# The opening of a decoder-block kernel, rebuilt: column sums by matmul, two tiles loaded in pieces, 13 short constant products

## The chip, the core and the metric

One core of a Trainium2 chip runs one program. Its engines work at the same time and wait for one another by semaphores: PE (TensorE, matmuls; PEld is its weight load), DVE (VectorE), ACT (ScalarE), POOL (GpSimd) and SP (SyncE, which here only issues DMAs). The metric is the device time of one execution in microseconds (us), as the median of several runs. Lower is better.

## The reference, cut to what matters

One decoder block on 256 tokens of width 2048, all in float32:

```python
mod = silu(c) @ w_ada + b_ada                 # (1, 6 * 2048)
sh1, sc1, g1, sh2, sc2, g2 = split(mod, 6)
h = rms_norm(x, norm1_g) * (1 + sc1) + sh1    # (256, 2048)
proj = h @ w_in                               # (256, 6144): q, k, v, gb, gc, xt
...                                           # attention, short convolution, w_out,
...                                           # then a gated ConvFFN with w_ffn_up, w_ffn_down
```

The change touches only the way to the first product of `h @ w_in`: the first 256 columns of `sc1` and `sh1`, the transposed normed x, and the first weight tile.

## The kernel before

Weights come from HBM in tiles of 1 MB ("raw", 128 rows x 2048 floats). All of them are issued by SP in one fixed order into a ring of buffers, so they land in that order: x (two tiles), four tiles of `w_ada` for the opening (the scale's columns 0 to 255 in two tiles of 8 row blocks, then the shift's), then the first weight tile of `w_in` in two halves, and from there `w_in` tiles with `w_ada` tiles between them. The `w_ada` tiles of the opening go through PE (L396, `ada<-raw,crep`), later ones through PE or through DVE (L387 and L389).

A product that is nearly exact in float32 is made of three fast ones: each weight tile is split into a rounded part `hi` (ACT, L329) and a rest `lo` (DVE, `lo<-raw,hi`), each h chunk into `h` and its rest, and PE computes hi·h, hi·(rest of h) and lo·h. The work is cut into slots, one weight tile each; slot 0 is `mc`, slot 1 `mv`, slot 2 `mg`, slot 3 `mx`, slots 4 and 5 `mq`. Within a slot hi comes first. Slots 0 to 4 multiply the first two h chunks (columns 0 to 255 of x), slot 5 is the first that needs chunks 2 and 3, whose parts are named `h` and `hl`. Each engine carries out its instructions in program order. The trace shows two passes (x16) for eight float32 products through `ada`, which the order of the instructions shows as x8. The splits of a slot stand two slots ahead of it.

The opening (L1470 to L1560): PE transposes x (`xn<-ident,xr`). DVE multiplies each transposed pair by the inverse norm (`xn_norm`, `xnT<-xn,n1rT`, eight of them). PE sums silu(c) times the scale's tiles into four groups of 32 rows (`Ada.consume`); ACT copies the sums out (`adae`, `Ada.evac`), PE transposes the copy and DVE adds the four groups up (`adac`, `adaz`, `Ada.cols`). The shift takes the same way after it. Then `hf` (DVE) is the normed x scaled, and `h` (ACT) is `hf` plus the shift column `z`, rounded. The first product `mc` needs `h` and the first piece of `hi`. In the program text `hf` stands behind all eight `xn_norm`.

Of the kernel before, what the change touches and what calls it, by code (L numbers as in the profile page):

```python
# [28 lines left out]
SH1, SC1, G1, SH2, SC2, G2 = range(6)  # L29
# [118 lines left out]
def tile_block(  # L148
# [22 lines left out]
    V, W = Vector(), nc.vector  # L171
# [5 lines left out]
    const = ctx.enter_context(tc.tile_pool(name="const", bufs=1))  # L177
# [4 lines left out]
    def bank(name):  # L182
        return ps.tile([P, 512], F32, tag="b", bufs=8, name=name)
# [30 lines left out]
    ident = const.tile([P, P], F32, name="ident")  # L214
# [3 lines left out]
    onesr = const.tile([P, P], F32R, name="onesr")  # L218
# [121 lines left out]
    crep = const.tile([P, NK, 32], F32, name="crep")  # L340
    A1 = const.tile([P, NK], F32, name="A1")
# [4 lines left out]
    class Ada:  # L346


        def __init__(self, part, c0, n, pe):
            self.part, self.c0, self.n, self.pe = part, c0, n, pe  # L350
            self.rows = 2048 // n
            self.tiles = NK // self.rows
            self.nch = n // P
            self.acc = None
            self.two = []
            self.used = 0

        def want(self, r):
            a = self.part * D + self.c0 * P
            k0 = r * self.rows  # L360

            def issue(t):
                nc.sync.dma_start(self.view(t), w_ada[0, k0 * P:(k0 + self.rows) * P, a:a + self.n]
                                  .rearrange("(k p) f -> p k f", p=P))
            return issue

        def home(self):
            what = f"ada{self.part}_{self.c0}"
            self.acc = sb.tile([P, 4, 512], F32, tag="raw", bufs=N_RAW, name=what).rearrange("p a b -> p (a b)")

            nc.gpsimd.memset(self.acc, 0.0)
            a = self.part * D + self.c0 * P
            nc.gpsimd.dma_start(self.acc[0:1, :], b_ada[0:1, a:a + self.n])
# [114 lines left out]
    hT = {}  # L488
# [31 lines left out]
    for w in CFG["parked"]:  # L520
        q = sb.tile([P, 4, 512], F32, tag="raw", bufs=N_RAW, name="pa_" + w)
# [15 lines left out]
    slots_begun = []  # L537

    def pair_load(k, f):
        def issue(t):  # L540

            n = 1 if not slots_begun else 2
            slots_begun.append(f)
            for j in range(0, 2, n):
                nc.sync.dma_start(t.rearrange("p (k h) f -> p k (h f)", k=2)[:, j:j + n],
                                  w_in[0, (k + j) * P:(k + j + n) * P, COL[f] * 512:COL[f] * 512 + 1024]
                                  .rearrange("(k p) f -> p k f", p=P))
        return issue


# [125 lines left out]
    for n, (f, part, k) in enumerate(seq):  # L676
# [6 lines left out]
        i = len(slots)  # L683
# [411 lines left out]
    for n, (what, *a) in enumerate(CFG["plan"]):  # L1095
        if what == "x":
# [10 lines left out]
            rest = todo  # L1107
# [12 lines left out]
    parts = []  # L1120
    for fs in CFG["down_turns"]:
        k = ka
# [46 lines left out]
        ready_at.update({(g.part, g.c0 + k): s + 2 for k in range(g.nch)})  # L1169

    ada_init = [Ada(SC1, 0, 256, True), Ada(SH1, 0, 256, True)]

    def h_chunks(ks):
        assert all((part, k) in done for k in ks for part in (SC1, SH1))

        for k in ks[::2]:
            t, hi, lo = t2k("hf"), t2k(f"h{k}", F32R), t2k(f"hl{k}", F32R)
            for j in range(2):
                s = slice(j * 256, (j + 1) * 256)
                act(t[:, s], xnT[k // 2][:, s], AF.Identity, scale=A1[:, k + j:k + j + 1], bias=B1[:, k + j:k + j + 1])  # L1180
                hT[k + j] = hi[:, s], lo[:, s]
            act(hi, t, AF.Copy)
            V.tensor_tensor(out=lo, in0=t, in1=hi.bitcast(F32), op=ALU.subtract)
# [268 lines left out]
    for i in range(len(slots)):  # L1452
# [3 lines left out]
        w = [("w", n) for n in ahead(i)]  # L1456
# [11 lines left out]
    for t in range(2):  # L1468
        r = sb.tile([P, 4, 512], F32, tag="hi", bufs=N_HL, name="xr").rearrange("p a b -> p (a b)")
# [16 lines left out]
    xnT, xnP = {}, {}  # L1486
# [26 lines left out]
    def xn_norm(*js):  # L1513
        for j in js:
            xnT[j] = t2k(f"xnT{j}")
            V.tensor_tensor(out=xnT[j].rearrange("p (k t) -> p k t", k=2), in0=xnP.pop(j).rearrange("p (k t) -> p k t", k=2),
                            in1=rT.unsqueeze(1).to_broadcast([P, 2, 256]), op=ALU.mult)

    xn_norm(0, 1, 2, 3)
    ada_init[0].consume(1)  # L1520
    ada_init[0].evac()
    ada_init[0].cols()
    xn_norm(4)
    xn_tr(5)
    ada_init[1].consume(0)
    xn_tr(6, 7)
    xn_norm(5, 6, 7)
    ada_init[1].consume(1)
    ada_init[1].evac()

    w = take(("w", 0))
    hi, lo = (sb.tile([P, 4, 512], F32R, tag=g, bufs=N_HL, name=g) for g in ("hi", "lo"))
    parts = [(slice(2 * k, 2 * k + 2), t1k("hf"), t2k(f"h{k}", F32R)) for k in range(2)]
    b1 = SH1 * NK
    for k, (s, h, hk) in enumerate(parts):
        hT[k] = halves(hk)
        V.tensor_scalar(h, xnT[0][:, k * 256:(k + 1) * 256], A1[:, k:k + 1], bcol[:, b1 + k:b1 + k + 1],
                        op0=ALU.mult, op1=ALU.add)  # L1540
    s = parts[0][0]
    if CFG["first_hi"]:
        V.tensor_copy(hi[:, s], w[:, s])
    else:
        act(hi[:, s], w[:, s], AF.Copy)
    z, _ = ada_init[1].cols(True)
    for k, (s, h, hk) in enumerate(parts):
        act(hT[k][0], h, AF.Identity, bias=z[:, k:k + 1])
# [38 lines left out]
    for i in range(len(slots)):  # L1587
# [28 lines left out]
        hi, lo = splits.pop(0)  # L1616
# [42 lines left out]
```

## Time and profile before

| | |
|---|---|
| median of three runs (lowest to highest) | 1145.96 us (1145.74 to 1147.56) |
| the profiled execution: its time, its span from first to last instruction | 1145.98 us, 1144.2 us |
| mean granted TensorE clock | 0.997 |
| bytes read from HBM, mean rate | 343.70 MB, 317 GB/s over the span |

Times in the trace count from the span's start; what lies around the span is 1145.98 − 1144.2 = 1.8 us. "PEclk" in a row is the share of the TensorE clock that was granted in that stretch. "DMA" is the mean busy share of the 16 DMA engines. A bracket behind a row gives the engine's idle time before it and what ended it. In the last column of a DMA row stands the time from the issue to the landing, in us.

### The profile page before, as it was taken

To read this page: it belongs to the slowest core of one execution; us is meant where nothing else is said; L and a number is where in the kernel's file an instruction comes from. 1 tells how busy PE (TensorE), PEld (TensorE's weight loads), DVE (VectorE), ACT (ScalarE), POOL (GpSimd) and SP (SyncE) were. 2 spreads that over 40 slices of the span, in tenths; PEclk is the share of its full clock that TensorE was granted. 3 is DMA by queue.
4 is the path that set the end of the run, shared out by engine and by line. 5 is a ranking of instruction groups with operands and counts; after the bars stand their busy time and mean duration, and the time that the engine had idled before them with its cause. 6 is when DMAs were issued, how large, how long until landed. Compare 5 with 4: busy or idle time off the path is not lost.

```text
span 1144.2 us, 16252 instructions
## 1 busy us (share of the span) xinstructions
PE 1129.7 (99%) x6035; PEld 954.1 (83%) x6035; DVE 1064.4 (93%) x1167; ACT 731.6 (64%) x1091; POOL 61.5 (5%) x90
## 2 busy tenths in 40 slices
PE   6999999999999999999999999999999999999998
PEld 4777778888888879988888888888888888888887
DVE  4789989989999998889999999899999999999798
ACT  4644455576786555566687676776677768866731
POOL 1000000000000000000000000101011101111000
PEclk8999999999999999999999999999999999999999
DMA  9999998998998899987679887999899988999951
GB/s 361 407 412 397 412 371 302 408 382 308 331 397 314 290 317 359 325 278 245 213 246 369 305 293 248 310 360 299 313 272 340 317 317 265 351 313 303 367 222 74
DMA packets 198687, 363.66 MB, mean 318 GB/s; under 512 B 9408, under 2 KB 108180, under 8 KB 194000
## 3 DMA queue, kind: packets, MB, share of 16 engines
q1 hardware_dynamic: 189152, 343.44, 82.8%
q0 software_dynamic: 8160, 17.04, 6.9%
q10 hardware_dynamic: 1296, 2.16, 0.6%
q8 instruction: 47, 0.77, 0.2%
q14 instruction: 32, 0.26, 0.1%
HBM read 343.70 MB, written 18.89 MB: 317 GB/s over the span
## 4 chain that ended last, share of the span: by engine, by line
PE 94%; DVE 2%; DMA 2%; issue 1%; ACT 1%; SPq 0%; DVEq 0%; ACTq 0%
PE z L1063 24%; PE z L1066 13%; PE u L1002 4%; PE u L1004 4%; PE u L1000 4%; PE z L1048 4%; PE ada L396 1%; DVE lo L166 1%; PE mx L516 1%; PE mq L516 1%; PE mg L516 1%; PE mk L516 1%; PE mx L517 1%; PE mv L516 1%; PE mg L517 1%; PE mq L517 1%
## 5 line engine op out<-in xcount | busy, mean ns | idle before, releaser
L329 ACT ACTIVATE hi<-raw 128x2048 fp32r<-128x2048 f32 (+1 forms) x227 | 417.6, 1857 | 263.6 <-DMA raw<-in_w_in_dram 73.5
L166 DVE TENSOR_TENSOR lo<-raw,hi 128x2048 fp32r<-128x2048 f32 (+2 forms) x229 | 501.6, 2200 | 23.3 <-ACT hi L329 23.1
L1063 PE MATMUL z<-h,hi 128*128 128x512 f32 x1280 | 303.3, 390 | 0.3 <-DVE ub L166 0.3
L1063 PEld LDWEIGHTS z<-h,hi 128*128 128x128 f32 x1280 | 237.8, 188 | 49.5 <-ACT hi L329 0.8
L389 DVE SCALAR_TENSOR_TENSOR ada<-raw,csil,ada 128x512 f32<-128x512 f32 (+3 forms) x167 | 195.7, 1175 | 5.3 <-DMA raw<-in_w_ada_dram 1.8
L1066 PEld LDWEIGHTS z<-h,lo 128*128 128x128 f32 x1280 | 163.1, 191 | 5.6
L1066 PE MATMUL z<-h,lo 128*128 128x256 f32 x1280 | 165.0, 283 | 0.0
L1002 PE MATMUL u<-hi,gh 128*128 128x512 f32 x224 | 88.1, 394 | 0.1
L1004 PE MATMUL u<-hi,gl 128*128 128x512 f32 x224 | 87.7, 392 | 0.0
L1000 PE MATMUL u<-lo,gh 128*128 128x512 f32 x224 | 61.4, 390 | 0.0
L812 ACT ACTIVATE uy<-ub,fc,fc 128x256 f32<-128x256 f32 x88 | 47.6, 599 | 11.9 <-DVE ub L166 11.9
L944 POOL DMA_DIRECT2D down_sums<-pu x42 | 36.7, 1290 | 304.3 <-ACT pu L940 304.3
L1002 PEld LDWEIGHTS u<-hi,gh 128*128 128x128 f32 x224 | 42.2, 188 | 10.0 <-ACT pu L940 2.9
L1000 PEld LDWEIGHTS u<-lo,gh 128*128 128x128 f32 x224 | 41.9, 188 | 9.2 <-DVE lo L166 0.3
L1004 PEld LDWEIGHTS u<-hi,gl 128*128 128x128 f32 x224 | 42.2, 189 | 7.5
L1048 PE MATMUL z<-h,hi 128*128 128x256 f32 x256 | 46.6, 284 | 0.4 <-ACT h L771 0.2
L823 ACT ACTIVATE tap<-ub,fc 128x256 f32<-128x256 f32 x96 | 41.7, 504 | 0.0
L1048 PEld LDWEIGHTS z<-h,hi 128*128 128x128 f32 x256 | 40.0, 192 | 0.8 <-ACT h L771 0.5
L166 DVE TENSOR_TENSOR ub<-z,ub 128x256 f32<-128x256 f32 x96 | 33.8, 414 | 7.2 <-ACT ub L844 7.1
L301 DVE TENSOR_TENSOR raw<-raw 128x1024 f32<-128x1024 f32 x32 | 38.9, 1217 | 1.2 <-DMA raw<-in_w_ffn_down_dram 1.2
L844 ACT ACTIVATE ub<-z 128x256 f32<-128x256 f32 x96 | 28.6, 383 | 12.7 <-PE z L1063 12.7
L1048 PE MATMUL z<-h,lo 128*128 128x256 f32 x128 | 36.2, 283 | 0.0
(460 smaller groups left out, 1787.3 us busy)
## 6 DMA issues: line engine op xcount, KB each, us to landing
raw<-in_w_ada_dram SPq DMA_DIRECT2D x96, 1024.0 KB, 7.4
raw<-in_w_ffn_up_dram SPq DMA_DIRECT2D x176, 512.0 KB, 6.1
raw<-in_w_in_dram SPq DMA_DIRECT2D x47, 1024.0 KB, 8.1
raw<-in_w_ffn_down_dram SPq DMA_DIRECT2D x44, 1024.0 KB, 9.5
raw<-in_w_out_dram SPq DMA_DIRECT2D x16, 1024.0 KB, 5.9
raw<-in_w_ffn_down_dram SPq DMA_DIRECT2D x32, 512.0 KB, 4.9
down_sums<-pu POOLq DMA_DIRECT2D x56, 256.0 KB, 8.0
raw<-in_w_ffn_down_dram SPq DMA_DIRECT2D x32, 256.0 KB, 5.3
```

What stands on the lines that cost most here:

```text
L166: f(*a, **k)
L329: act(hi[:, :n], t[:, :n], AF.Copy)
L389: W.scalar_tensor_tensor(out=self.acc, in0=t[:, j, :], scalar=csil[:, i:i + 1], in1=self.acc, op0=ALU.mult, op1=ALU.add)
L516: mm(o, a, hi[:, k, s], start=(first and k == 0), stop=False)
L812: act(y[:, s], b[:, s], AF.Identity, bias=bias[:, i + j:i + j + 1], scale=w[2][:, i + j:i + j + 1])
L823: act(z[:, s], b[:, s], AF.Copy, scale=w[2 - d][:, i + j:i + j + 1])
L1000: mm(bank_of(key), a, lo[:, n], start=False, stop=j in ends)
L1002: mm(bank_of(key), a, hi[:, n], start=key not in begun, stop=False)
L1004: mm(bank_of(key), b, hi[:, n], start=False, stop=False)
L1048: mm(o, w[:, j, a], h2T[k + j][:, v * 256:v * 256 + 256], start=begins and j == 0 and w is hi and not v, stop=ends and j == 3 and w is lo)
L1063: mm(zp[grp][ft], hi[:, j, ft * P:(ft + 1) * P], h2T[k + j], start=begins and j == 0, stop=ends and j == 3 and not late)
L1066: mm(zp[grp][ft][:, :256], lo[:, j, ft * P:(ft + 1) * P], h2T[k + j][:, :256], start=False, stop=ends and j == 3 and late)
```

## The change

1. **Column sums of the shift.** Before: ACT copies the sums out, PE transposes two blocks of 128 x 128, DVE adds four columns of each, and ACT adds the result to `hf`. Now: ACT copies the sums out, PE multiplies the copy by a 0/1 column `sel` (two matmuls of one column each, into the bank `one`), DVE copies the two columns to `z`, and the first `h` is made by DVE, the second by ACT. `sel` is made at the start by one DVE reduction.
2. **Last shift tile in two DMAs** of four row blocks each, and its 8 products in two groups of four, each behind its own DMA.
3. **First weight tile in four DMAs** of 128 x 512 instead of two of 128 x 1024, and its `hi` in four casts by ACT, DVE, ACT, DVE instead of two.
4. **13 constant products** of 128 x 128 (`onesr` by itself, into an unused part of `one`): nine behind the first scale tile, four behind the second.
5. **DVE's order.** `hf` stands behind the second `xn_norm` instead of behind the eighth, and the eighth `xn_norm` stands behind the casts.

First place, PE from the first scale tile (`ada<-raw,crep`) to the scale's transposes (`adac`); `n1b` spreads the inverse norm over the partitions, `one<-onesr` are the constant products. Before:

```order
L396 MATMUL ada_0_165<-raw,crep 32x256 x8
L1509 MATMUL n1b<-n1d,ones 128x128 x2
L396 MATMUL ada_0_165<-raw,crep 32x256 x8
L453 MATMUL adac_0_206<-ident,adae_0_203 128x128 x2
L1495 MATMUL xn_214<-ident,xr 128x128 x4
```

The same stretch of PE now:

```order
L416 MATMUL ada_0_170<-raw,crep 32x256 x8
L1532 MATMUL one<-onesr 128x128 x9
L1541 MATMUL n1b<-n1d,ones 128x128 x2
L416 MATMUL ada_0_170<-raw,crep 32x256 x8
L1532 MATMUL one<-onesr 128x128 x4
L473 MATMUL adac_0_221<-ident,adae_0_218 128x128 x2
L1519 MATMUL xn_237<-ident,xr 128x128 x4
```

Nine constant products came in ahead of `n1b` and four ahead of `adac`; the rest stands as it stood.

Second place, PE from the last transposes of x to the first products of slot 0 (`mc`), before:

```order
L1495 MATMUL xn_233<-ident,xr 128x128 x2
L396 MATMUL ada_0_219<-raw,crep 32x256 x8
L453 MATMUL adac_0_268<-ident,adae_0_256 128x128 x2
L583 MATMUL mc_293<-hi,h_261 128x512
L583 MATMUL mc_294<-hi,h_261 128x512
```

The same stretch now (`one<-sel,adae` are the new column sums):

```order
L1519 MATMUL xn_256<-ident,xr 128x128 x2
L381 MATMUL ada_0_242<-raw,crep 32x256 x8
L1575 MATMUL one<-sel,adae 128x1 x2
L606 MATMUL mc_313<-hi,h_285 128x512
L606 MATMUL mc_314<-hi,h_285 128x512
```

The two transposes of 128 x 128 became two products of one column; PE's list is the same from `mc` on.

Third place, DVE from the scale's column sums (`adaz<-adac`) to the rests of the first two h chunks (the rows `h_261<-hf,adaz,h_261` and its like), before:

```order
L166 TENSOR_REDUCE adaz<-adac_0_206 128x2
L166 SCALAR_TENSOR_TENSOR adaz<-adaz,vbc 128x2
L166 TENSOR_TENSOR A_90<-adaz,vbc 128x2
L166 TENSOR_TENSOR xnT_212<-xn_139,n1rT 128x512
L166 TENSOR_TENSOR xnT_240<-xn_214,n1rT 128x512
L166 TENSOR_TENSOR xnT_242<-xn_230,n1rT 128x512
L166 TENSOR_TENSOR xnT_244<-xn_233,n1rT 128x512
L166 TENSOR_SCALAR hf<-xnT_185,A_90,vbc 128x256 x2
L166 CAST hi<-raw 128x1024
L166 TENSOR_REDUCE adaz<-adac_0_268 128x2
L166 SCALAR_TENSOR_TENSOR h_261<-hf,adaz,h_261 128x256
L166 SCALAR_TENSOR_TENSOR h_263<-hf,adaz,h_263 128x256
```

The same stretch now, up to the rest of the first chunk:

```order
L168 TENSOR_REDUCE adaz<-adac_0_221 128x2
L168 SCALAR_TENSOR_TENSOR adaz<-adaz,vbc 128x2
L168 TENSOR_TENSOR A_92<-adaz,vbc 128x2
L168 TENSOR_SCALAR hf<-xnT_200,A_92,vbc 128x256 x2
L168 TENSOR_TENSOR xnT_231<-xn_138,n1rT 128x512
L168 TENSOR_TENSOR xnT_233<-xn_141,n1rT 128x512
L168 TENSOR_TENSOR xnT_235<-xn_144,n1rT 128x512
L168 TENSOR_TENSOR xnT_263<-xn_237,n1rT 128x512
L168 TENSOR_TENSOR xnT_265<-xn_253,n1rT 128x512
L168 COPY adaz<-one 128x2
L168 TENSOR_SCALAR h_285<-hf,adaz 128x256
L168 SCALAR_TENSOR_TENSOR h_285<-hf,adaz,h_285 128x256
```

`hf` went ahead of five `xnT`, so five of them stand between it and the shift's sums; the cast of `hi` went behind the sums, which are a plain copy now, and the first rounded `h` is made on DVE.

The core of the diff:

```diff
+       'busy': [9, 4, 0],
+       'norm_at': [2, 7, 8],
...
+    sel = const.tile([P, 1], F32, name="sel")
+    V.tensor_reduce(out=sel, in_=ident.rearrange("p (j r) -> p j r", j=4)[:, :, 0], axis=AX.X, op=ALU.add)
...
             def issue(t):
-                nc.sync.dma_start(self.view(t), w_ada[0, k0 * P:(k0 + self.rows) * P, a:a + self.n]
-                                  .rearrange("(k p) f -> p k f", p=P))
+                for i, j in self.cuts.get(r, [(0, self.rows)]):
+                    nc.sync.dma_start(self.view(t)[:, i:j], w_ada[0, (k0 + i) * P:(k0 + j) * P, a:a + self.n]
+                                      .rearrange("(k p) f -> p k f", p=P))
...
+        def products(self, r, i, j):
+            if i == 0:
+                self.used += 1
+                self.held = self.view(take((self, r)))
...
+            for k in range(i, j):
+                q = 32 * (k % 4)
+                mm(self.acc[q:q + 32, :], crep[:, self.rows * r + k, :], self.held[:, k, :],
+                   start=r == 0 and k < 4, stop=r == self.tiles - 1 and k >= self.rows - 4,
+                   tile_position=(0, q))
+            if j == self.rows:
+                load_next()
...
-            n = 1 if not slots_begun else 2
-            slots_begun.append(f)
-            for j in range(0, 2, n):
...
+            if not slots_begun:
+                slots_begun.append(f)
+                for j in range(4):
+                    a = (COL[f] + j % 2) * 512
+                    nc.sync.dma_start(t[:, j], w_in[0, (k + j // 2) * P:(k + j // 2 + 1) * P, a:a + 512])
+                return
...
+    ada_init[1].cuts[1] = [(0, 4), (4, 8)]
...
+    def keep_busy(b, n):
+        for _ in range(n):
+            mm(b[:, 256:384], onesr, onesr, start=True, stop=True)
+
+    p_one = bank("one")
+    w0, w1, w2 = CFG["busy"]
+    keep_busy(p_one, w0)
     pr = bank("n1b")
...
-    xn_norm(0, 1, 2, 3)
-    ada_init[0].consume(1)
-    ada_init[0].evac()
-    ada_init[0].cols()
-    xn_norm(4)
+    xn_norm(*range(n0))
+    sc.consume(1)
+    keep_busy(p_one, w1)
+    sc.evac()
+    sc.cols()
+    hf = []
+    b1 = SH1 * NK
+    for k in range(2):
+        hf.append(t1k("hf"))
+        V.tensor_scalar(hf[k], xnT[0][:, k * 256:(k + 1) * 256], A1[:, k:k + 1], bcol[:, b1 + k:b1 + k + 1],
+                        op0=ALU.mult, op1=ALU.add)
+    xn_norm(*range(n0, 5))
     xn_tr(5)
-    ada_init[1].consume(0)
+    sh.products(0, 0, 8)
     xn_tr(6, 7)
-    xn_norm(5, 6, 7)
-    ada_init[1].consume(1)
-    ada_init[1].evac()
+    xn_norm(*range(5, n1))
+    sh.products(1, 0, 4)
+    keep_busy(p_one, w2)
+    sh.products(1, 4, 8)
+    rows_sum = t2k("adae")[:, :256]
+    act(rows_sum, sh.acc, AF.Copy)
+    for k in range(2):
+        mm(p_one[:, k:k + 1], rows_sum[:, k * P:(k + 1) * P], sel, start=k == 0, stop=k == 1)
+    z = small(8, "adaz")[:, :2]
+    V.tensor_copy(z, p_one[:, :2])
...
-    z, _ = ada_init[1].cols(True)
-    for k, (s, h, hk) in enumerate(parts):
-        act(hT[k][0], h, AF.Identity, bias=z[:, k:k + 1])
-        if not k:
-            act(hi[:, parts[1][0]], w[:, parts[1][0]], AF.Copy)
...
+    act(hi[:, 0], w[:, 0], AF.Copy)
+    for k in range(2):
+        hT[k] = halves(hk[k])
+        if k:
+            act(hT[k][0], hf[k], AF.Identity, bias=z[:, k:k + 1])
+        else:
+            V.tensor_scalar(hT[k][0], hf[k], z[:, k:k + 1], None, op0=ALU.add)
...
+    rest(0)
+    V.tensor_copy(hi[:, 1], w[:, 1])
+    rest(1)
+    act(hi[:, 2], w[:, 2], AF.Copy)
+    V.tensor_copy(hi[:, 3], w[:, 3])
+    xn_norm(*range(n1, n2))
```

More of the change, by code (lines that the diff above doesn't have):

```diff
@@ L356, in __init__ @@
             self.used = 0
+            self.cuts = {}
         def want(self, r):
@@ L362, in issue @@
             def issue(t):
-                nc.sync.dma_start(self.view(t), w_ada[0, k0 * P:(k0 + self.rows) * P, a:a + self.n]
-                                  .rearrange("(k p) f -> p k f", p=P))
-            return issue
+                for i, j in self.cuts.get(r, [(0, self.rows)]):
+                    nc.sync.dma_start(self.view(t)[:, i:j], w_ada[0, (k0 + i) * P:(k0 + j) * P, a:a + self.n]
+                                      .rearrange("(k p) f -> p k f", p=P))
+            return issue
+        def products(self, r, i, j):
+            if i == 0:
+                self.used += 1
+                self.held = self.view(take((self, r)))
+            if self.acc is None:
+                self.acc = bank(f"ada{self.part}_{self.c0}")[:, :self.n]
+            for k in range(i, j):
[5 more added lines that the diff above has]
+                load_next()
         def home(self):
@@ L540, in issue @@
         def issue(t):
-            n = 1 if not slots_begun else 2
-            slots_begun.append(f)
-            for j in range(0, 2, n):
-                nc.sync.dma_start(t.rearrange("p (k h) f -> p k (h f)", k=2)[:, j:j + n],
-                                  w_in[0, (k + j) * P:(k + j + n) * P, COL[f] * 512:COL[f] * 512 + 1024]
-                                  .rearrange("(k p) f -> p k f", p=P))
+            if not slots_begun:
[4 more added lines that the diff above has]
+                return
+            nc.sync.dma_start(t.rearrange("p (k h) f -> p k (h f)", k=2),
+                              w_in[0, k * P:(k + 2) * P, COL[f] * 512:COL[f] * 512 + 1024]
+                              .rearrange("(k p) f -> p k f", p=P))
         return issue
@@ L1517, in xn_norm @@
                             in1=rT.unsqueeze(1).to_broadcast([P, 2, 256]), op=ALU.mult)
-    xn_norm(0, 1, 2, 3)
-    ada_init[0].consume(1)
-    ada_init[0].evac()
-    ada_init[0].cols()
-    xn_norm(4)
+    sc, sh = ada_init
+    n0, n1, n2 = CFG["norm_at"]
+    xn_norm(*range(n0))
[9 more added lines that the diff above has]
+                        op0=ALU.mult, op1=ALU.add)
@@ L1533, in tile_block @@
+    V.tensor_copy(z, p_one[:, :2])
     w = take(("w", 0))
     hi, lo = (sb.tile([P, 4, 512], F32R, tag=g, bufs=N_HL, name=g) for g in ("hi", "lo"))
-    parts = [(slice(2 * k, 2 * k + 2), t1k("hf"), t2k(f"h{k}", F32R)) for k in range(2)]
-    b1 = SH1 * NK
-    for k, (s, h, hk) in enumerate(parts):
[L1538 to L1545, printed above, removed]
-    z, _ = ada_init[1].cols(True)
-    for k, (s, h, hk) in enumerate(parts):
-        act(hT[k][0], h, AF.Identity, bias=z[:, k:k + 1])
-        if not k:
-            act(hi[:, parts[1][0]], w[:, parts[1][0]], AF.Copy)
-    for k, (s, h, hk) in enumerate(parts):
-        V.scalar_tensor_tensor(out=hT[k][1], in0=h, scalar=z[:, k:k + 1], in1=hT[k][0].bitcast(F32),
-                               op0=ALU.add, op1=ALU.subtract)
@@ L1554, in tile_block, with rest @@
-    for s, _, _ in parts:
-        V.tensor_tensor(out=lo[:, s], in0=w[:, s], in1=hi[:, s].bitcast(F32), op=ALU.subtract)
+    done.update((SH1, k) for k in range(2))
+    hk = [t2k(f"h{k}", F32R) for k in range(2)]
+    act(hi[:, 0], w[:, 0], AF.Copy)
[5 more added lines that the diff above has]
+            V.tensor_scalar(hT[k][0], hf[k], z[:, k:k + 1], None, op0=ALU.add)
+    def rest(k):
+        V.scalar_tensor_tensor(out=hT[k][1], in0=hf[k], scalar=z[:, k:k + 1], in1=hT[k][0].bitcast(F32),
+                               op0=ALU.add, op1=ALU.subtract)
@@ L1556, in tile_block @@
+    rest(0)
[4 more added lines that the diff above has]
+    xn_norm(*range(n1, n2))
+    for j in range(0, 4, 2):
+        V.tensor_tensor(out=lo[:, j:j + 2], in0=w[:, j:j + 2], in1=hi[:, j:j + 2].bitcast(F32), op=ALU.subtract)
+    xn_norm(*range(n2, 8))
     splits.append((hi, lo))
```

## The prediction, made before the changed kernel was run

> **What bounds the kernel now.** First the page's first part, then PE's waits from 28.1 us to the end:
>
> ```profile
> PE 1129.7 (99%) x6035; PEld 954.1 (83%) x6035; DVE 1064.4 (93%) x1167; ACT 731.6 (64%) x1091; POOL 61.5 (5%) x90
> ```
>
> ```profile
> PE z L1063 <- DVE ub L166: 0.3, 1, 0.3
> PE z L1048 <- ACT h L771: 0.2, 1, 0.2
> ```
>
> PE waits 0.5 us in 1116 us, so the end should move with every microsecond that the opening gives back, unless something stands just behind PE. Next the opening, cut where the granted clock changed, and one stretch behind it (length, busy us and count of PE, PEld, DVE, ACT, POOL; clock, DMA share, GB/s):
>
> ```profile
> 11.01:14.43 3.42, 1.60 (x21) 0.81 (x19) 1.30 (x7) 2.08 (x5) 2.35 (x5) 1.00 1.09 385
> 14.43:17.84 3.41, 2.96 (x20) 1.40 (x20) 1.86 (x4) 0.77 (x2) 0.00 (x0) 0.50 1.09 379
> 21.26:24.67 3.41, 1.82 (x17) 0.85 (x10) 2.45 (x7) 1.79 (x4) 0.00 (x0) 1.00 1.03 416
> 24.67:28.08 3.41, 3.41 (x9) 2.65 (x8) 2.84 (x4) 2.35 (x3) 0.00 (x0) 0.50 1.03 399
> 28.08:31.50 3.42, 3.42 (x16) 2.82 (x15) 3.17 (x2) 2.84 (x3) 0.00 (x0) 1.00 1.08 385
> ```
>
> The clock changes in steps of 3.41 us. A stretch with PE busy 1.60 of 3.42 (47%) or 1.82 of 3.41 (53%) is followed by one at half clock, one with 2.96 of 3.41 (87%) by full clock. The half-clock stretch in slot 0 does 9 products where the next does 16: 7 of 16 of 3.42 us, 1.5 us lost.
>
> The way to the first product, from the timeline:
>
> ```profile
> 20.73 1.07 PE L396 MATMUL ada<-raw,crep 128*32 128x256 f32 x16
> 21.82 0.73 DVE L166 TENSOR_SCALAR hf<-xnT,A,vbc 128x256 f32<-128x256 f32 x2
> 21.86 0.38 ACT L417 ACTIVATE adae<-ada 128x256 f32<-128x256 f32 x1 [4.02 <-PE ada L396]
> 22.30 0.44 PE L453 MATMUL adac<-ident,adae 128*128 128x128 f32 x2 [0.50 <-ACT adae L417]
> 22.46 0.69 DVE L166 CAST hi<-raw 128x1024 fp32r<-128x1024 f32 x1
> 23.06 0.16 DVE L166 TENSOR_REDUCE adaz<-adac 128x2 f32<-128x8 f32 x1
> 23.26 0.51 ACT L1548 ACTIVATE h<-hf,adaz 128x256 fp32r<-128x256 f32 x1 [1.01 <-DVE adaz L166]
> 23.82 0.50 PE L583 MATMUL mc<-hi,h 128*128 128x512 f32 x1 [1.08 <-ACT h L1548]
> ```
>
> The sums are ready on PE at 22.74 and stand behind the cast until 23.06; `mc` starts at 23.82. Then the transfers: issues of the last shift tile and of the first weight tile's halves with their times to landing, and the DMA engines from 2.5 to 77 us:
>
> ```profile
> 9.56 2.63 SPq L363 DMA_DIRECT2D raw<-in_w_ada_dram  x1
> ...
> raw<-in_w_ada_dram SPq DMA_DIRECT2D x1, 1024.0 KB, 10.8
> ...
> 12.24 2.71 SPq L545 DMA_DIRECT2D raw<-in_w_in_dram  x1
> ...
> raw<-in_w_in_dram SPq DMA_DIRECT2D x1, 512.0 KB, 9.4
> ...
> 14.99 0.43 SPq L545 DMA_DIRECT2D raw<-in_w_in_dram  x1
> ...
> raw<-in_w_in_dram SPq DMA_DIRECT2D x1, 512.0 KB, 7.9
> ...
> 2.50:77.00 74.50, 66.58 (x364) 48.17 (x365) 51.58 (x73) 40.42 (x54) 5.57 (x11) 0.95 1.04 403
> ```
>
> Landings at 20.36, 21.64 and 22.89. At a share of 1.04 the DMA engines are full up to 77 us: a tile lands when the bytes ahead of it are through, whatever PE does. Since byte count and order stay, I look for places before 77 us where PE stands just behind a tile. Slot 5 is the closest: ACT's split, DVE's `lo` and column sums behind it, and ACT's `hf`, `h`, DVE's `hl`, and PE's two weight loads that read them:
>
> ```profile
> 49.60 1.92 ACT L329 ACTIVATE hi<-raw 128x2048 fp32r<-128x2048 f32 x1 [1.14 <-DMA raw<-in_w_in_dram]
> 51.55 2.29 DVE L166 TENSOR_TENSOR lo<-raw,hi 128x2048 fp32r<-128x2048 f32 x1 [0.23 <-ACT hi L329]
> ...
> 54.42 1.09 ACT L1180 ACTIVATE hf<-xnT,B,A 128x256 f32<-128x256 f32 x2 [0.44 <-DVE A L166]
> 55.55 0.63 ACT L1182 ACTIVATE h<-hf 128x512 fp32r<-128x512 f32 x1
> ...
> 56.21 0.69 DVE L166 TENSOR_TENSOR hl<-hf,h 128x512 fp32r<-128x512 f32 x1 [1.82 <-ACT h L1182]
> ...
> 56.94 0.19 PEld L516 LDWEIGHTS mq<-hi,h 128*128 128x128 f32 x1 [0.84 <-ACT h L1182]
> 57.05 0.19 PEld L517 LDWEIGHTS mq<-hi,hl 128*128 128x128 f32 x1
> ```
>
> From a landing near 49.5 to `hl` at 56.90 everything follows without a gap that PE could shorten, and PE loads `hl` at 57.05. It can be 0.10 us earlier there (0.05 for the hand-over), hardly more. Slot 2's `w_ada` tile (issue, time to landing, use on PE) lands at 41.74 and is used at 43.30: with a hand-over of 0.1 us, a lead of at most 1.4 us passes it.
>
> ```profile
> 29.44 3.04 SPq L363 DMA_DIRECT2D raw<-in_w_ada_dram  x1
> ...
> raw<-in_w_ada_dram SPq DMA_DIRECT2D x1, 1024.0 KB, 12.3
> ...
> 43.30 0.12 PEld L396 LDWEIGHTS ada<-raw,crep 128*32 128x32 f32 x3 [0.35 <-issue]
> ```
>
> Behind 77 us there is one more such place, slot 24:
>
> ```profile
> 90.21 0.16 DVE L166 SCALAR_TENSOR_TENSOR adaz<-adaz,vbc 128x4 f32<-128x4 f32 x1 [0.18 <-ACT ada L460]
> ...
> 94.05:163.80 69.75, 69.75 (x327) 54.08 (x326) 69.01 (x70) 27.34 (x39) 0.00 (x0) 1.00 1.03 400
> ...
> 171.71 0.19 PEld L516 LDWEIGHTS mq<-hi,h 128*128 128x128 f32 x1 [0.20 <-ACT hi L329]
> ```
>
> DVE is busy 69.01 of 69.75 us, and the split at its end lets PE load at 171.71 after 0.20 us of waiting. Ahead of that stretch DVE idled 0.18 us for ACT, which followed PE's transposes: that much can PE's lead shorten.
>
> **The change, part by part.** The profiled execution took 1145.98 us (span 1144.2), the runs' median is 1145.96: the sum from the one holds for the other.
>
> *Last shift tile in pieces, sums by matmul, less in front of them.* The last half lands at 20.36. Its eight passes take some 0.65 us (of 1.07 for 16, most of the last pass is its tail): 21.1 with a hand-over. ACT copies in 0.38: 21.5. The two one-column products have no row; the ends are 0.44 (the transposes they replace) and 1.15 (`n1b`, two products of 128 columns at half clock, next fence). The former is nearer, since nothing but a weight load remains: 22.0. A copy like the 0.16 reduction, an add like one `hf` (0.37): `mc` at 22.7, 1.1 us earlier, 0.4 with the other end. `sel` is one small DVE reduction in the first microseconds, while DVE waits for x: nothing.
>
> ```profile
> 14.38 1.15 PE L1509 MATMUL n1b<-n1d,ones 128*128 128x128 f32 x4 [1.11 <-DVE n1d L166]
> 15.98 2.48 DVE L166 TENSOR_TENSOR xnT<-xn,n1rT 128x512 f32<-128x512 f32 x4 [1.55 <-ACT n1rT L1511]
> 18.38 0.16 DVE L166 TENSOR_REDUCE adaz<-adac 128x2 f32<-128x8 f32 x1
> 19.70 1.09 PE L1495 MATMUL xn<-ident,xr 128*128 128x128 f32 x8
> ```
>
> *The new wait on DVE.* The copy stands behind `hf` and five `xnT`. If the scale's sums come at 18.38 as now, three small ones, `hf` (0.73) and five `xnT` at 0.62 end at 22.8, and `mc` starts at 23.4: 0.4 us earlier. If the clock holds from 14.43, PE's 20 passes there take half their time, the scale comes over 1 us sooner, and the copy waits for PE, not DVE. Behind the copy on DVE stand the first `h`, its rest and two casts, and PE waits for all of them.
>
> *Constant products.* By the eight transposes in 1.09 us one takes 0.12 to 0.14 us, nine some 1.1 to 1.2 us, in the 1.11 us that PE idles ahead of `n1b`; four take 0.5. Ends: nothing, or twice that at half clock (`n1b` up to 1.2 us late), which the DVE queue would pass on. PE's share of 11.01 to 14.43 rises from 1.60 to 2.7 of 3.42 (79%), between 53% and 87%: I take the clock as held. With `mc` at 22.7 the share of 21.26 to 24.67 is about 2.4 of 3.41 (70%), as uncertain; if it holds, 1.5 us more.
>
> *First weight tile in pieces.* Its first quarter lands near 21.0, ahead of need, and the last quarter near 22.9 is needed 12 products after 22.7. `lo` stands behind one more `xnT` (0.62), and behind 16 products (3.4 us) on PE: hidden.
>
> *The transfers.* Three more DMAs for the same bytes. The two halves took 1.28 and 1.25 us, together 2.53; a tile at 403 GB/s takes 2.60. So a cut costs nothing visible; the far end is SP's 0.43 us for each, 1.3 us, if the transfers had to wait for it. SP issues some 8 to 11 us ahead of the landing (the rows of the landings), so later issues are not late. No gain is possible: bytes and order are the same. I take +0.1.
>
> *Sum.* PE leads by 0.4 to 2.6 us behind slot 0. At most 1.4 pass slot 2, 0.1 slot 5, and at most 0.2 slot 24; the rest becomes waits on PE. −0.2 from the lead, +0.1 from the later tiles: 1145.98 − 0.1 = 1145.9.
>
> [...]
>
> **The rivals.** *Slower: a new half-clock stretch.* PE now waits up to 1.3 us ahead of slot 5 (the 1.4 of lead less 0.1). If that falls within one 3.41 us stretch, PE is busy 62% there. It decides at the share where the clock drops, between 53% and 87%. Price 1.5 us, and PE then stands behind its tiles, so nothing absorbs it: 1145.9 + 1.5 = 1147.4. For: the share is nearer 53%. Against: the stretch's edge may cut the wait in two. *Faster: the lead passes.* For: PE's own waits are 0.5 us. Then 1.1 + 1.5 = 2.6 us: 1143.4. Against: the rows of slots 5 and 24, which need the same bytes first. *The tiles come late*: three pieces at 0.43 us push slot 5 by 1.3: 1147.1. *The constant products don't hold the clock*: `mc` at 23.4 and slot 0 at half clock; the 0.4 us of lead still exceeds slot 5's 0.1: 1145.9 as well.
>
> **How the numbers follow.** The lead absorbed, with or without the clock held: 0.62 (0.15 of it without), 1145.3 to 1146.4 by the ends of the small terms. New half-clock stretch 0.18, late tiles 0.08, the whole lead 0.06, about 1 us of it 0.06 (1144.9). 1145.0 to 1147.6 leaves out the last two and the tail of the second. 0.2% is 2.3 us, about what a measurement of this kernel can tell from no change. Faster by that (under 1143.7) is the whole lead: 0.06. Slower (over 1148.3) needs two new half-clock stretches or one and late tiles: 0.03. Within: 0.91.
>
> **What would show it.** Right: `mc` starts at 22.7 to 23.4; PE has new idle time ahead of slot 2's second `w_ada` tile or in slot 5, released by DMA, ACT `h` or DVE `hl`; `hl` of slot 5 ends at 56.9 to 57.1; PE at 172 us stands within 0.3 us of its old place. Wrong: `hl` of slot 5 over half a microsecond earlier, tiles landing earlier or over half a microsecond later, half clock behind 31 us, or a lead at 172 us that is near the one at 28 us.

## The result, and the profile after

| | kernel before | changed kernel |
|---|---|---|
| median of six runs (lowest to highest) | 1145.95 us (1145.18 to 1147.56) | 1152.95 us (1152.75 to 1153.53) |
| profiled execution: its time, its span | 1145.98 us, 1144.2 us | 1152.75 us, 1150.9 us |

The ratio is 1.0057 with a 95% interval from 1.0047 to 1.0068: the kernel became about 0.6% slower. The forecast was 1145.9 us and its range ended at 1147.6.

The page's first part and PE's waits from 28.1 us to the end, changed kernel (in the waits: us in total, times, longest):

```profile
PE 1132.3 (98%) x6050; PEld 955.1 (83%) x6050; DVE 1065.2 (93%) x1170; ACT 731.2 (64%) x1091; POOL 61.4 (5%) x90
```

```profile
PE ada L416 <- DMA raw<-in_w_ada_dram: 1.6, 3, 1.0
PE u L1027 <- DVE gl L168: 0.7, 1, 0.7
PE mg L536 <- ACT pa_v L551: 0.6, 1, 0.6
PE mx L536 <- ACT pa_g L551: 0.6, 1, 0.6
PE mv L536 <- DVE pa_x L168: 0.6, 1, 0.6
```

Before, PE waited 0.5 us in all behind 28.1 us. Now it waits 5.0 us (the longest rows are shown), for transfers first, then for engines that a late transfer has held up. The stretch from 2.5 to 77 us (the columns of the prediction's windows) says why:

```profile
2.50:77.00 74.50, 64.13 (x358) 46.76 (x359) 48.94 (x73) 40.09 (x54) 3.46 (x7) 0.98 1.04 379
```

The DMA engines are as full as before (1.04) and move 379 GB/s instead of 403. What took 74.5 us at 403 takes 74.5 × 403 / 379 = 79.2 us now, 4.7 us more; the tile that landed at 77.29 us before lands at 82.06. The chain of slot 5 and the load of slot 24, from the timelines of ACT, DVE and PE's weight loads, stand beside the prediction's rows:

```profile
53.05 1.92 ACT L333 ACTIVATE hi<-raw 128x2048 fp32r<-128x2048 f32 x1 [1.10 <-DMA raw<-in_w_in_dram]
...
59.66 0.69 DVE L168 TENSOR_TENSOR hl<-hf,h 128x512 fp32r<-128x512 f32 x1 [1.82 <-ACT h L1206]
...
176.78 0.19 PEld L536 LDWEIGHTS mq<-hi,h 128*128 128x128 f32 x1 [0.23 <-ACT hi L333]
```

The split that stood at 49.60 us behind its tile stands at 53.05, `hl` moved from 56.21 to 59.66, both by 3.45 us, and the load of slot 24 from 171.71 to 176.78, by 5.07 us. The durations are unchanged and the inner gaps nearly so: the chain came later as a whole, with its tile. Matched product by product, PE is 0.2 us early at `mc`, 1.9 us late at slot 3, 5.0 us late from slot 13 to 750 us, and loses another 0.4 us near 755 us and 1.1 us at 990 us, which makes 6.4 us of the 6.7 by which the span grew. At 990 us a product waits for `gl`, which DVE made late behind a `w_ffn_down` tile that it had waited for.

The slow transfers begin ahead of the tiles that the change cut. Clock stretches of the opening:

```profile
10.26:13.67 3.41, 2.25 (x27) 1.50 (x26) 1.03 (x7) 2.35 (x5) 2.62 (x6) 1.00 1.09 348
13.67:17.08 3.41, 2.94 (x33) 2.12 (x32) 1.55 (x4) 0.77 (x2) 0.00 (x0) 1.00 1.11 340
...
20.50:23.91 3.41, 1.93 (x22) 0.97 (x14) 2.02 (x6) 1.41 (x3) 0.00 (x0) 1.00 1.06 393
23.91:27.32 3.41, 3.41 (x10) 2.62 (x9) 2.77 (x6) 0.63 (x1) 0.00 (x0) 0.50 1.01 406
```

348 and 340 GB/s stand against 385 and 379 in the prediction's first two clock stretches of the kernel before. In them land tiles that the change left whole. The trace lists the packets one by one: between 28 and 77 us a packet of 1 KB took 46.0 ns before and 50.9 ns now, one of 2 KB 84.2 and 88.0, one of 4 KB 159.5 and 165.0. In the mean a packet costs some 4 to 6 ns more, whatever its size. Single packets don't pay alike: before, all of the 3556 packets of 1 KB took 46 ns; now 1095 of 4067 still do, and most of the others take 47 to 60. The whole stretch before, then now:

```profile
28.00:77.00 49.00, 49.00 (x248) 36.24 (x247) 39.92 (x46) 27.84 (x36) 2.10 (x4) 1.00 1.05 408
```

```profile
28.00:77.00 49.00, 45.83 (x226) 33.45 (x225) 37.32 (x45) 29.52 (x37) 0.00 (x0) 1.00 1.05 385
```

(Two executions among the experiments were disturbed and are left out, the profiled one of before_gap32 with 4006 us and one of the kernel before with 2286 us.)

**Theory S.** The new tile `sel` holds 4 bytes a partition and occupies 32. It is allocated ahead of nearly everything, so every later buffer moved by 32 bytes: in the built programs the ring of weight tiles started at byte 30208 (59 × 512) of each partition and starts at 30240. Packets that start off some boundary are dearer. **Rival P:** the tiles in pieces upset the queue. **Rival Q:** the constant products, or the new order, do it.

### The profile page after: what moved, and what is told of

The parts are those of the page before. It is cut to its first block, busy times and chain, and to the rows that moved or that the text cites. A ratio compares the mean times of both kernels' runs of the same rounds, so it can differ in the third digit from the quotient of the medians.

```text
span 1150.9 us, 16291 instructions
## 1 busy us (share of the span) xinstructions
PE 1132.3 (98%) x6050; PEld 955.1 (83%) x6050; DVE 1065.2 (93%) x1170; ACT 731.2 (64%) x1091; POOL 61.4 (5%) x90
## 3 DMA queue, kind: packets, MB, share of 16 engines
q1 hardware_dynamic: 189456, 343.44, 84.3%
## 4 chain that ended last, share of the span: by engine, by line
PE 80%; DMA 9%; DVE 8%; issue 1%; ACT 1%; SPq 0%; DVEq 0%; ACTq 0%
PE z L1086 21%; PE z L1089 11%; DVE lo L168 5%; PE z L1071 4%; DMA raw<-in_w_ada_dram 4%; PE u L1023 4%; PE u L1025 3%; PE u L1027 3%; DMA raw<-in_w_in_dram 3%; DMA raw<-in_w_ffn_up_dram 1%; PE mv L536 1%; PE mv L534 1%; DMA raw<-in_w_ffn_down_dram 1%; PE mv L537 1%; PE mq L536 1%
## 5 line engine op out<-in xcount | busy, mean ns | idle before, releaser
L1089 PE MATMUL z<-h,lo 128*128 128x256 f32 x1280 | 165.0, 283 | 0.0
L1027 PE MATMUL u<-hi,gl 128*128 128x512 f32 x224 | 87.9, 392 | 0.7 <-DVE gl L168 0.7
```

Source lines behind the costliest of these rows:

```text
L1027: mm(bank_of(key), b, hi[:, n], start=False, stop=False)
L1089: mm(zp[grp][ft][:, :256], lo[:, j, ft * P:(ft + 1) * P], h2T[k + j][:, :256], start=False, stop=ends and j == 3 and late)
```

## The experiments

Names that begin with "before" are the kernel before with unused tiles, each of which adds one short memset on POOL (before_raw8k adds none); "packed" is the changed kernel with `sel` in spare bytes. Packet times are means over 28 to 77 us in the trace.

| kernel | weight tiles start, modulo 256 | 1 KB, 2 KB, 4 KB packet, ns | median us | ratio to before (95%) |
|---|---|---|---|---|
| after_packed | 0 | 46.0, 84.3, 159.3 | 1147.28 | 1.0009 (0.9999 to 1.0018) |
| before_gap32 | 32 | not measured | 1151.72 | 1.0049 (1.0032 to 1.0066) |
| after_whole | 32 | 51.0, 88.0, 165.2 | 1152.04 | 1.0057 (1.0040 to 1.0074) |
| before_gap64 | 64 | 51.2, 88.0, 165.4 | 1152.26 | 1.0050 (1.0035 to 1.0065) |
| before_gap128 | 128 | 51.3, 88.3, 165.5 | 1152.94 | 1.0058 (1.0043 to 1.0073) |
| before_gap256 | 0 | 46.0, 84.2, 159.5 | 1146.05 | 0.9997 (0.9988 to 1.0006) |
| before_gaplate | 0 | 46.0, 84.2, 159.6 | 1159.76 | 1.0115 (1.0100 to 1.0130) |
| before_raw8k | 0 | 46.0, 84.2, 159.6 | 1146.50 | 1.0001 (0.9991 to 1.0010) |
| before_rawonly32 | 32 | 51.0, 87.9, 165.4 | 1151.84 | 1.0043 (1.0027 to 1.0058) |
| before_gaplate256 | 0 | 46.0, 84.2, 159.5 | 1146.52 | 1.0005 (0.9991 to 1.0018) |

The medians are of four runs each, of three for before_gap32, and of ten for after_packed, before_gap256, before_raw8k and before_gaplate256. The median of the kernel before was 1146.31 to 1146.46 us in these comparisons.

### The shift taken out: after_packed

```diff
-    sel = const.tile([P, 1], F32, name="sel")
+    spare = const.tile([P, 8], F32, name="spare")
+    sel, ssA = spare[:, 2:3], spare[:, :2]
...
-    ssA = const.tile([P, 2], F32, name="ssA")
```

> The changed kernel with its 0/1 column placed in unused bytes of another constant, so that the new 32-byte tile is gone and all buffers that DMAs fill start at multiples of 512 bytes again, as before the change; every instruction is kept. Theory S (the 32-byte shift makes every DMA packet dearer): packets of 1 KB at 46 ns and of 4 KB at 159 ns between 28 and 77 us as before, the tile that landed at 77.29 us before and at 82.06 us in the changed kernel lands at 77.0 to 77.8, and the time is 1145.0 to 1146.5 us. Rival P (the tiles cut in pieces slow the DMA queue): no change, 1152 to 1153.5 us, packets at 51 and 164 ns. Rival Q (the constant products or the new order of DVE and ACT do it): 1152 to 1153.5 us as well.

The window from 28 to 77 us, here and in the fences like it that follow:

```profile
28.00:77.00 49.00, 48.19 (x242) 34.93 (x241) 39.69 (x46) 27.72 (x36) 2.10 (x4) 1.00 1.05 408
```

408 GB/s, the tile of 77.29 us lands at 77.03, and the median is back at 1147.28 us, 0.8 us above the range that theory S gave but no longer told apart from the kernel before. Rivals P and Q fall as the cause of the slow transfers: pieces, constant products and order are all still in it. Of the 7.0 us, 5.7 went with the 32 bytes.

### The shift alone: before_gap32

```diff
+    gap = const.tile([P, 1], F32, name="gap", padded_shape=[P, 8])
+    nc.gpsimd.memset(gap, 0.0)
```

> The kernel before with one unused constant of 32 bytes (and one memset of it on POOL in the opening) at the place where the change put its 0/1 column; nothing else is changed. Theory S: packets of 1 KB at 51 ns and of 4 KB at 164 ns, tiles 4 to 5 us later by 80 us, 1151 to 1153.5 us. Rivals P and Q: 1145.5 to 1146.5 us, packets at 46 and 159 ns.

1151.72 us, as theory S said. 32 unused bytes make the kernel before half a percent slower.

### The pieces taken out, the shift left: after_whole

```diff
-    ada_init[1].cuts[1] = [(0, 4), (4, 8)]
...
-                for j in range(4):
-                    a = (COL[f] + j % 2) * 512
-                    nc.sync.dma_start(t[:, j], w_in[0, (k + j // 2) * P:(k + j // 2 + 1) * P, a:a + 512])
+                for j in range(2):
+                    nc.sync.dma_start(t.rearrange("p (k h) f -> p k (h f)", k=2)[:, j:j + 1],
+                                      w_in[0, (k + j) * P:(k + j + 1) * P, COL[f] * 512:COL[f] * 512 + 1024]
+                                      .rearrange("(k p) f -> p k f", p=P))
```

> The changed kernel with the last shift tile in one DMA and the first weight tile in two, as before; the 0/1 column stays in its own 32 bytes. Theory S: still 1151.5 to 1154 us, with packets at 51 and 164 ns. Rival P: 1145.5 to 1147 us. Rival Q: 1152 to 1154 us, packets as short as before (46 and 159 ns).

```profile
28.00:77.00 49.00, 46.56 (x230) 34.03 (x229) 37.48 (x46) 28.64 (x37) 0.00 (x0) 1.00 1.05 385
```

Still 385 GB/s and 1152.04 us: the pieces are not what costs.

### How coarse the boundary is: before_gap64, before_gap128, before_gap256, before_raw8k

The edit is that of before_gap32 with `padded_shape` 16, 32 and 64. In before_raw8k three constants stand behind the buffers, so that the weight tiles start at 24576 and at multiples of 8192 from there; no instruction is added:

```diff
+    late = ctx.enter_context(tc.tile_pool(name="late", bufs=1))
+    for _ in range(16):
+        small(8, "place")
+    for _ in range(N_RAW):
+        sb.tile([P, 4, 512], F32, tag="raw", bufs=N_RAW, name="place")
...
-    ident = const.tile([P, P], F32, name="ident")
+    ident = late.tile([P, P], F32, name="ident")
```

> The kernel before with an unused constant of 64 bytes instead of 32 in the same place. Theory S says only that some multiple of bytes is the limit: if packets are dear unless their target starts at a multiple of 64 bytes, 1145.5 to 1146.5 us; if the limit is 128, 256 or 512 bytes, 1150 to 1153.5 us. Rivals P and Q: 1145.5 to 1146.5 us.

> The kernel before with an unused constant of 128 bytes where the 32-byte one stood; all buffers that DMAs fill start at 128 modulo 512. Shifts of 32 and 64 bytes cost 5 to 6 us alike. If a packet is dear unless it starts at a multiple of 128 bytes: 1145.5 to 1147 us and 400 to 410 GB/s between 28 and 77 us. If the limit is 256 or 512: 1150 to 1153 us and 380 to 390 GB/s.

> The same with an unused constant of 256 bytes. Limit of 256 bytes or less: 1145.5 to 1147 us, 400 to 410 GB/s between 28 and 77 us. Limit of 512: 1150 to 1153 us, 380 to 390 GB/s. I hold 256 or less for the likelier, since it is a half of the smallest row that the kernel loads in a tile (1 KB) and no row ends up split in more 512-byte pieces by a shift of 256 than by one of 64.

> The kernel before with its constants and buffers placed so that every weight tile starts at a multiple of 8192 bytes instead of 512; no instruction is changed. If a still coarser start makes packets cheaper yet: 1 KB packets under 45 ns, over 412 GB/s between 28 and 77 us and 1140 to 1145 us. If the limit lies at 512 or below: 1145.5 to 1147 us, 46 and 159 ns. The second is the likelier.

The window of before_gap128:

```profile
28.00:77.00 49.00, 46.56 (x229) 33.97 (x228) 38.34 (x47) 28.59 (x37) 0.00 (x0) 1.00 1.05 386
```

And that of before_gap256:

```profile
28.00:77.00 49.00, 48.13 (x240) 34.58 (x239) 39.63 (x46) 27.72 (x36) 2.10 (x4) 1.00 1.05 408
```

Shifts of 32, 64 and 128 bytes cost the same; 256 costs nothing, and multiples of 8192 bring nothing more than multiples of 256. Of the starts tried, the multiples of 256 are the cheap ones. (The expectation for 256 bytes took them for half of a 1 KB row; they are a quarter, and the run decides without that argument.)

### Whose address it is: before_gaplate, before_rawonly32

In before_gaplate a tile of 32 bytes stands behind the weight tiles, x and `hi`, ahead of `lo`, `h` and the rest:

```diff
         xr.append(r)
+    gap = sb.tile([P, 8], F32, tag="gap", bufs=1, name="gap")
+    nc.gpsimd.memset(gap[:, :1], 0.0)
```

> The kernel before with an unused constant of 32 bytes placed behind the buffers that DMAs fill (weight tiles and x stay at multiples of 512) and ahead of the others, so that only the targets and operands of the engines shift by 32 bytes. Theory S (the packets' targets): no change, 1145.5 to 1147 us, 400 to 410 GB/s between 28 and 77 us. Rival E (the engines' reads and writes of shifted buffers collide with the DMA's writes or become slower): 1150 to 1153 us.

The window from 100 to 240 us of the kernel before, then of before_gaplate:

```profile
100.00:240.00 140.00, 140.00 (x644) 112.33 (x637) 133.96 (x118) 71.33 (x142) 2.56 (x2) 1.00 0.97 377
```

```profile
100.00:240.00 140.00, 140.00 (x630) 110.23 (x630) 132.54 (x118) 70.08 (x142) 2.56 (x2) 1.00 0.97 374
```

Neither had this: 1159.76 us, 13 us more. The transfers do what theory S says (46.0 ns, 409 GB/s from 28 to 77 us), but PE, busy all the time at full clock, gets through 630 products where it got through 644. The trace has most products of `hi` following one another by 231 to 236 ns instead of 226 or 227. It is another effect than the changed kernel's, most of whose products keep 226 and 227 ns. So the time of this run doesn't separate the theories; that of the next does. before_rawonly32 shifts the weight tiles alone and leaves `hi`, `lo`, `h` and x at multiples of 256:

```diff
     vcb = t1k("vcb")
+    gap = sb.tile([P, 8], F32, tag="gap", bufs=1, name="gap")
+    nc.gpsimd.memset(gap[:, :1], 0.0)
...
+    gap2 = sb.tile([P, 56], F32, tag="gap2", bufs=1, name="gap2")
+    nc.gpsimd.memset(gap2[:, :1], 0.0)
     xr = []
```

> The kernel before with two unused tiles, one of 32 bytes ahead of the ring of weight buffers and one of 224 bytes behind it: the weight tiles start at 32 modulo 256, everything behind them (x, hi, lo, h and the rest) stays at multiples of 256. Theory S (what counts is the start of a DMA's target): 1150.5 to 1153 us, 380 to 390 GB/s between 28 and 77 us. Rival E (the engines' operands count): 1145.5 to 1147 us, 400 to 410 GB/s.

```profile
28.00:77.00 49.00, 45.87 (x226) 33.30 (x225) 38.32 (x46) 28.52 (x37) 0.00 (x0) 1.00 1.05 385
```

385 GB/s and 1151.84 us: shifting the weight tiles alone brings the loss, by the transfers. The engines that read the shifted tiles show next to nothing: the 195 splits `lo<-raw,hi` take 2284 ns in the kernel before and in the changed one, and 2287 here.

### What slowed PE: before_gaplate256

The edit is that of before_gaplate with 64 instead of 8 columns (256 bytes).

> As the kernel with 32 unused bytes behind the weight tiles and hi, but with 256: hi starts at 0 and lo, h and the rest at 256 modulo 512. In the kernel with 32 bytes there the matmuls of hi followed one another by 231 to 236 ns instead of 226 or 227, and the time was 13 us longer. If what slowed them is that hi and h start differently modulo 256: 227 ns and 1145.5 to 1147.5 us here. If it is any difference modulo 512: 231 to 236 ns and 1155 to 1160 us. If it is the unused tile itself, or the place in memory: 1155 to 1160 us.

```profile
100.00:240.00 140.00, 140.00 (x644) 112.73 (x639) 133.88 (x119) 71.67 (x142) 2.56 (x2) 1.00 0.97 377
```

644 products again, most at 226 and 227 ns, and 1146.52 us. Neither an unused tile at that place nor a difference of 256 bytes slows PE; one of 32 between `hi` and what stands behind it does, while a shift of both by 32 (the changed kernel) doesn't. Which operands must agree, and modulo what, wasn't tried further.

### What the rest of the change is worth: packed_nobusy, packed_plain

```diff
-       'busy': [9, 4, 0],
+       'busy': [0, 0, 0],
```

> The changed kernel with the 0/1 column in spare bytes (1147.28 us, a ratio of 1.0009 to the kernel before) and without its 13 constant products. Theory A (the opening's lead of half a us or so is swallowed behind the DMA's stretch, and nothing else in it matters): 1145.5 to 1147.5 us, a ratio of 0.999 to 1.001, whatever the clock does in the opening. Rival B (the constant products bring on the half clock in slot 0, seen in all three profiles of the changed kernel so far, and cost about 1 us): 1145 to 1146 us, no half clock behind 20 us, a ratio under 0.9995. Rival C (they hold the clock): half clock at 14 us as in the profile of before, 1146.5 to 1148 us.

packed_plain takes the edit of after_whole as well.

> The same, and with the last shift tile in one DMA and the first weight tile in two as before: only the column sums and the order of DVE and ACT are left of the change. Theory A: 1145.5 to 1147.5 us, a ratio of 0.999 to 1.001, and the first product mc 0.2 to 0.7 us later than with the pieces. Rival B: as the run without the constant products. Rival P2 (the pieces cost on their own, by the gap of 2 us ahead of the third piece of the first weight tile): 0.3 to 1 us less than the run with the pieces.

1146.90 us (12 runs), ratio 1.0004 (0.9995 to 1.0013), and 1145.81 us (11 runs), ratio 0.9996 (0.9985 to 1.0006): the same as the kernel before, as theory A said. The first product in after_packed, packed_nobusy, packed_plain, and last in before_raw8k, whose opening is the old one:

```profile
21.95 4.34 PE L607 MATMUL mc<-hi,h 128*128 128x512 f32 x11 [0.73 <-ACT h L1587]
```

```profile
21.88 4.34 PE L607 MATMUL mc<-hi,h 128*128 128x512 f32 x11 [0.73 <-ACT h L1587]
```

```profile
22.43 3.89 PE L608 MATMUL mc<-hi,h 128*128 128x512 f32 x16 [0.73 <-ACT h L1587]
```

```profile
22.21 2.18 PE L588 MATMUL mc<-hi,h 128*128 128x512 f32 x8 [0.80 <-ACT h L1553]
```

With x landing within 0.1 us of one another, the rebuilt opening starts `mc` 0.3 us sooner, by the pieces: with them it gains 0.5 us, without them `mc` is 0.2 us later than in the old opening. The constant products do nothing for it. The clock of packed_nobusy around the start of `mc`, then that of before_raw8k and that of packed_plain:

```profile
19.27:22.68 3.41, 2.17 (x24) 1.31 (x17) 2.63 (x8) 1.50 (x4) 0.00 (x0) 1.00 1.05 408
22.68:26.10 3.42, 3.42 (x10) 2.65 (x9) 3.27 (x5) 1.05 (x2) 0.00 (x0) 0.50 1.03 422
```

```profile
12.43:15.84 3.41, 1.87 (x22) 1.13 (x23) 2.21 (x8) 0.77 (x2) 0.15 (x1) 1.00 1.10 380
15.84:19.26 3.42, 2.78 (x30) 1.80 (x29) 3.35 (x9) 0.00 (x0) 0.00 (x0) 1.00 1.09 395
19.26:22.67 3.41, 1.97 (x20) 0.91 (x20) 2.71 (x7) 0.89 (x2) 0.00 (x0) 1.00 1.03 416
22.67:26.08 3.41, 3.23 (x14) 2.20 (x13) 1.54 (x3) 2.05 (x3) 0.00 (x0) 1.00 1.02 421
```

```profile
10.91:14.32 3.41, 1.93 (x25) 1.18 (x28) 1.13 (x6) 1.43 (x3) 1.65 (x4) 1.00 1.09 383
14.32:17.74 3.42, 2.55 (x38) 1.40 (x30) 2.78 (x8) 0.64 (x2) 0.00 (x0) 1.00 1.09 382
```

Half clock in slot 0 came without constant products too, and the time isn't under 1146 us, so rival B falls. Without them packed_nobusy kept full clock from 9.03 to 22.68 us, so rival C falls.

Rival P2 said 0.3 to 1 us less without the pieces, and the medians differ by 1.1 us. The two traces put the difference elsewhere. Matched product by product, packed_nobusy is 1.06 us behind packed_plain at 28 us, with its half-clock stretch, but 0.10 at 42 us and 0.05 at 172 us. It is 2.0 us behind only at 800 us: at 750 us DVE waits 2.8 us for a `w_ffn_down` tile there and 0.3 us in packed_plain. So nothing that the pieces do in the opening lasts in these two executions. What makes that later tile late stays open, as does whether after_packed's 0.9 us over the kernel before is more than chance. No version beat the kernel before by an amount that these runs can tell.

## Why the prediction was wrong, point by point

**The transfers** is the step that failed. It read "No gain is possible: bytes and order are the same. I take +0.1", with 0 and 1.3 us for ends. It priced the number of DMAs and took the price of a packet as given. The runs show 4.7 us by 77 us, from the address that each packet is written to. Most of the price can be followed: the kernel before has 3556, 4096 and 1936 packets of 1, 2 and 4 KB between 28 and 77 us. With 4.9, 3.8 and 5.5 ns more for each, that is 43.6 us on 16 engines, 2.7 us of each; the stretch ahead of 28 us, where most packets are of 1 KB, gives 1.6 us by the same reckoning. That is 4.3 of the 4.7 us; the rest isn't accounted for. The cause stood in the diff as the line that makes `sel`. The prediction costed that as one DVE reduction, "nothing", and didn't ask what the tile moves.

The Trainium skill, "DMA: Bandwidth & Descriptors", section "How a descriptor splits into AXI transactions", says that a read transaction must start at a 256-byte boundary and that what doesn't start there begins with one at the boundary below. It is told there for reads; here the end that moved is the one written to. The boundary agrees with the runs, which put it above 128 and at no more than 256 bytes. The price does not go as the page's count of 32-byte beats: by that, as an estimate from the page, 1 KB starting 32 bytes past a boundary takes 33 beats and 128 bytes past it 36, 1 or 4 beats over 32, which is 1.4 or 5.8 ns of 46. Measured were 5.0 and 5.3. A price that hardly depends on the packet's size or on the shift would fit one more transaction for each packet, but that is argued and not shown: no run here counts transactions, and some packets pay nothing while others pay up to 14 ns.

**What bounds the kernel** was right. Slot 2's `w_ada` tile, slot 5 and slot 24 are the places where the late tiles pushed PE. From PE's timeline of the changed kernel, slot 2's second `w_ada` tile:

```profile
45.20 1.07 PE L416 MATMUL ada<-raw,crep 128*32 128x256 f32 x16 [0.96 <-DMA raw<-in_w_ada_dram]
```

The prediction used these places only to see how little a lead could pass; read the other way, they say that a microsecond of DMA lost ahead of 77 us is about a microsecond of the end, since PE had nothing to spare there.

**The lead absorbed** was right where it can be seen without the shift. The load of slot 24 in after_packed, then in before_raw8k:

```profile
171.23 0.19 PEld L537 LDWEIGHTS mq<-hi,h 128*128 128x128 f32 x1 [0.22 <-ACT hi L334]
```

```profile
170.94 0.19 PEld L521 LDWEIGHTS mq<-hi,h 128*128 128x128 f32 x1 [0.23 <-ACT hi L334]
```

The 0.3 us at `mc` are gone, but this pair alone doesn't show what took them: half clock in slot 0 made them 0.7 us of delay at 28 us, of which 0.3 are left here. The lead of 1.06 us that packed_plain has over packed_nobusy at 28 us, and that is down to 0.10 at 42 us, shows the absorption. The ratio of 1.0009 is inside the 0.2%.

**Less in front of `mc`** was forecast as 1.1 us and measured as 0.2 in the changed kernel. Its path, from the timeline:

```profile
21.11 0.64 PE L381 MATMUL ada<-raw,crep 128*32 128x256 f32 x8 [0.25 <-DMA raw<-in_w_ada_dram]
21.82 0.38 ACT L1573 ACTIVATE adae<-ada 128x256 f32<-128x256 f32 x1 [5.09 <-PE ada L381]
22.25 0.61 PE L1575 MATMUL one<-sel,adae 128*128 128x1 f32 x4 [0.50 <-ACT adae L1573]
22.90 0.16 DVE L168 COPY adaz<-one 128x2 f32<-128x2 f32 x1 [1.32 <-PE one L1575]
23.09 0.51 ACT L1587 ACTIVATE h<-hf,adaz 128x256 fp32r<-128x256 f32 x1 [0.37 <-DVE adaz L168]
23.59 1.35 PE L606 MATMUL mc<-hi,h 128*128 128x512 f32 x3 [0.73 <-ACT h L1587]
```

The last half landed at 21.07 instead of 20.36, a part of the slow transfers: 0.7 of the missing 0.9 us. From there to `mc` the forecast was 2.34 us, and 2.52 passed. The difference is the two column sums, 0.61 us where 0.44 was taken (of ends 0.44 and 1.15). The eight passes (0.64 for 0.65), the copy out (0.38), DVE's copy (0.16, released by PE and not by the `xnT` ahead of it) and its add (0.35 for 0.37; the profile puts `mc`'s wait down to ACT's `h`, which ends only at 23.60) came as worked out. A part of the forecast lead was also one execution's: in the profile of before x landed at 6.70 and 9.37 us, in before_raw8k at 5.62 and 8.45, and the old way from the last shift tile to `mc` took 3.46 us there and 2.86 here, of which the new one saves 0.3.

**The clock.** That the clock would hold behind the stretch of 11.01 to 14.43 came true: 13.67 to 17.08 ran at full clock in the changed kernel. The cause given didn't hold: PE was busy 66% of the stretch ahead of it, not 79%, and the prediction took half clock to follow stretches with PE busy 47% or 53%. In packed_plain full clock followed 1.93 of 3.41 (57%), and in the changed kernel half clock followed the same 1.93; in before_raw8k full clock followed 1.87 (55%) and 1.97 (58%), in packed_nobusy half clock followed 2.17 (64%). The share of one stretch does not decide. The Trainium skill ("TensorE: Matmul & The Clock Gate", "Why this matters for your kernels") tells authors to leave no PE-idle gaps over about 3 us, since one window of idle time takes the clock back to half. Such gaps are not the only cause here: in the changed kernel PE never idled over 1.6 us behind its first instruction, and half clock came. In before_raw8k it never did either, and none came. What decides stays open.

The half-clock stretch in slot 0, which the prediction priced at 1.5 us, was not a fixed part of the old opening either. Of its eight readable traces, two have one there (before and before_gap128); of the five traces of the new opening, four do (all but packed_plain). Between 31 us and the last product no half clock came: the first rival didn't happen.

**The rivals.** "The tiles come late" had the right course (slot 5 pushed, nothing absorbs it) and the wrong source: SP's issues for 1.3 us, where it was the packets for 5. The list of what would prove the forecast wrong named "tiles landing ... over half a microsecond later", and that is what came.

## What to carry to other kernels

A new constant is also a shift of everything allocated behind it: look at the start addresses of the buffers that DMAs fill before and after, and keep them at multiples of 256 bytes by placing small tiles in spare bytes or padding them. Where the DMA share stays at its limit while GB/s falls, compare the mean time of packets of one size before looking at the number or order of DMAs.

## What was not expected of the hardware

In the mean a packet costs about 5 ns more (46 to 51 ns for 1 KB, 84 to 88 for 2 KB, 159.5 to 165 for 4 KB) when its target starts 32, 64 or 128 bytes past a multiple of 256. The same buffers cost the engines next to nothing as operands (2284 to 2287 ns for a split). In the later part of the kernel (200 to 1140 us) the median of the 1 KB packets is 46 ns in the changed kernel as well, and the mean 50.3 against 48.1: why the shift is cheaper there isn't settled. And PE's products lost 2% of their pace (630 for 644 in 140 us) when `lo`, `h` and what stands behind them were moved by 32 bytes against `hi`, and none at 256.
